# SSD's output product as seven block products a pair, with its loads, ropes and attention's start re-ordered

## The chip, the cores and the metric

The kernel runs on one core of a Trainium2 chip. The metric is the device time of one execution in microseconds (us), lower is better. Five engines work side by side, each through its own instructions in order: TensorE (PE in the profile, its weight loads PEld), VectorE (DVE), ScalarE (ACT), GpSimd (POOL) and SyncE (SP), which in this kernel issues nearly all DMAs. They wait for each other by semaphores.

## The reference

One decoder layer on 1024 tokens of width 1024, all float32: a Mamba-2 state space mixer (SSD) and differential attention side by side, merged by gates, then a gated feed-forward part. What matters here:

```python
h = rms_norm(x, pre_norm1_w[layer]) * (1.0 + sc1) + sh1
proj = h @ w_in[layer]
z, xbc, dt_raw, q, k, v, gates = jnp.split(proj, IN_SPLITS, axis=-1)
y_ssd = ssd_branch(z, xbc, dt_raw, ...)          # normed y, times norm_w
y_att = diff_attention_branch(q, k, v, ...)      # q, k rotated by rope first
gate_ssd, gate_att = jnp.split(jax.nn.sigmoid(gates), N_BRANCH, axis=-1)
merged = gate_ssd * (y_ssd @ w_ssd_o[layer]) + gate_att * (y_att @ w_attn_o[layer])
```

The change concerns `y_ssd @ w_ssd_o`, a product of 1024 x 1024 by 1024 x 1024, and what stands around it.

## The kernel before

**Numbers in two parts.** Each float32 operand is kept as a high part (rounded to fp32r by ScalarE's copy) and a low part (the rest, by VectorE's subtraction); a product is three matmuls, high by high, high by low and low by high. Tiles named `hl` hold both parts of 128 channels x 512 tokens, 4 KB a partition. h, transposed, is sixteen such tiles `hT[k][half]`, k of 8 channel groups, half of two token halves. `block_half` computes 128 output channels for 512 tokens: 8 k x 3 = 24 matmuls of 128 x 512.

**Buffers.** `Slots` is a pool of 43 buffers of 4 KB a partition. `get` takes the one that has been free longest, `put` gives one back; whoever writes a reused buffer waits for its last reader. The weights have rings of their own: raw blocks 3 deep (`wraw`), high and low parts 4 deep each.

**Pairs.** Earlier in the kernel eight pairs of 128-wide weight blocks are computed by Winograd's form of Strassen's scheme (`pairs`, `x_mms`, `x_split`, `x_sum`, loop at L618 onward): the two weight blocks and the four quarters of h (two channel halves by two token halves) give seven block products instead of eight. Each product is a step p0 to p6 of 12 matmuls. Four weight sums a pair are made by VectorE, seven weight splits by ScalarE and VectorE, and the results are gathered from three PSUM banks: X takes p0, p2, p4, p6, Z takes p1, Y takes p3 and p5. X is copied out after p0 and after p2, while the next product into X waits its turn.

```python
order = (("b11", "X"), ("b21", "Z"), ("t2", "X"), ("t1", "Y"), ("t3", "X"), ("b22", "Y"), ("t4", "X"))
```

`x_ahead(m, p)` splits the weights three steps ahead and, at two places a pair, lets SP load the next raw block (`x_load`).

**The stage of this change** lies between the SSD scan and attention, inside one block whose order on TensorE, VectorE, ScalarE and SP is written by hand. First blocks 0 and 1 of q and k (`seq`, four of them) by `block_half`, in between `turn_y`: four transposes put 128 channels of y for 512 tokens into a PSUM bank, ScalarE scales it to the high part, VectorE makes the low part. The banks are taken in the fixed rotation wa, wb, wa, wc, with two buffers of wa, so a bank is used again by the fourth turn after. After the first half of a block comes the `rope` of the block before: ScalarE's copy out of the bank, VectorE's shuffle, GpSimd's product with the cosines, VectorE's product with the sines, their sum, the split, and 16 small stores to DRAM (`store_qk`). Then the loop over eight output blocks j: 48 matmuls each, `w_ssd_o` block split ahead, gate `gsd[j]` loaded, gate times product stored to `msd[j]`. At j = 3 and 4 the q and k tiles of the first two heads are loaded (`load_qk`).

**After it** attention: a stream of dense blocks (q, k blocks 3 to 7 and the attention gates, `dense_stream`) fills TensorE between scores, transposes and values of the heads. `fill(1)` emits three matmuls. The first 14 fills come before the first score. Its order is by hand on TensorE, VectorE, ScalarE and GpSimd, while SP's instructions are placed by the scheduler there.

## Time and profile before

| | us |
|---|---|
| median of 3 runs (lowest, highest) | 1852.3 (1850.74, 1853.15) |
| profiled execution, its own time | 1848.95 |
| its span, first to last instruction | 1847.1 |
| TensorE busy in it | 1822.4 (99%) |
| VectorE, ScalarE busy | 1294.9 (70%), 888.3 (48%) |
| GpSimd busy | 144.5 (8%) |
| granted TensorE clock, mean | 0.997 |

Busy time is the time in which an engine had an instruction in work. TensorE's instructions overlap: a 128x512 matmul is shown with some 389 ns and the next one starts long before its end, so the pace is read from starts. A row of the timeline reads: start, duration, engine, line of the kernel, operation, output<-inputs, count; in brackets the engine's idle time before it and who ended it. A row of a stretch gives from:to, its length, busy time of PE, PEld, DVE, ACT and POOL with counts, the granted clock, the DMA engines' busy share, and GB/s.

### The profile page before, as it was taken

To read this page: it belongs to the slowest core of one execution; us is meant where nothing else is said; L and a number is where in the kernel's file an instruction comes from. 1 tells how busy PE (TensorE), PEld (TensorE's weight loads), DVE (VectorE), ACT (ScalarE), POOL (GpSimd) and SP (SyncE) were. 2 spreads that over 40 slices of the span, in tenths; PEclk is the share of its full clock that TensorE was granted. 3 is DMA by queue.
4 is the path that set the end of the run, shared out by engine and by line. 5 is a ranking of instruction groups with operands and counts; after the bars stand their busy time and mean duration, and the time that the engine had idled before them with its cause. 6 is when DMAs were issued, how large, how long until landed. Compare 5 with 4: busy or idle time off the path is not lost.

```text
span 1847.1 us, 24410 instructions
## 1 busy us (share of the span) xinstructions
PE 1822.4 (99%) x8974; PEld 1527.3 (83%) x8974; DVE 1294.9 (70%) x1980; ACT 888.3 (48%) x1720; POOL 144.5 (8%) x128
## 2 busy tenths in 40 slices
PE   6999999999999999999999999999999999999998
PEld 4888899988888888888888888888888888888887
DVE  6777867799654257777667464487898888876545
ACT  6644543456532145565556232565545454455532
POOL 0000000266421000000000100000000000000001
PEclk9999999999999999999999999999999999999999
DMA  8365367687646856566734754122333222378744
GB/s 335 133 216 183 103 208 238 219 315 268 242 125 185 260 132 172 165 170 164 198 104 146 236 196 177 52 95 103 103 120 108 103 97 98 109 235 309 243 158 165
DMA packets 130217, 322.57 MB, mean 175 GB/s; under 512 B 14881, under 2 KB 38833, under 8 KB 130098
## 3 DMA queue, kind: packets, MB, share of 16 engines
q1 hardware_dynamic: 129138, 317.86, 52.3%
q0 software_dynamic: 960, 3.15, 0.5%
q8 instruction: 71, 1.16, 0.3%
q14 instruction: 48, 0.39, 0.1%
HBM read 225.79 MB, written 95.17 MB: 174 GB/s over the span
## 4 chain that ended last, share of the span: by engine, by line
PE 91%; DVE 4%; ACT 3%; issue 1%; DMA 1%; POOL 0%; SPq 0%; DVEq 0%; POOLq 0%; ACTq 0%
PE upx L1744 4%; PE upx L1743 4%; PE upx L1745 4%; PE o L1437 3%; PE dx L2108 2%; PE dx L2107 2%; PE dx L2106 2%; PE upy L1743 2%; PE upy L1744 2%; PE upy L1745 2%; PE v L950 2%; PE z L117 2%; PE z L118 2%; PE z L116 2%; PE dy L2108 2%; PE dy L2107 2%
## 5 line engine op out<-in xcount | busy, mean ns | idle before, releaser
L1743 PE MATMUL upx<-t,wu_t 128*128 128x512 f32 x264 | 103.2, 391 | 0.5 <-DVE cv L2171 0.4
L1744 PE MATMUL upx<-t,wu_t 128*128 128x512 f32 x264 | 102.9, 390 | 0.2 <-DVE t L1861 0.2
L1745 PE MATMUL upx<-t,wu_t 128*128 128x512 f32 x264 | 102.7, 389 | 0.0
L1717 ACT ACTIVATE wu_t<-sab 128x512 fp32r<-128x512 f32 x57 | 34.1, 627 | 128.3 <-DVE sab L1734 128.3
L1425 ACT COPY aT<-at 128x512 f32<-128x512 f32 (+2 forms) x96 | 46.0, 479 | 96.3 <-PE at L1424 96.3
L1437 PEld LDWEIGHTS o<-vt,aT 128*128 128x128 f32 x576 | 75.3, 191 | 9.2 <-ACT aT L1425 4.6
L95 DVE TENSOR_TENSOR g_lo<-gst,g_hi 128x1024 fp32r<-128x1024 f32 (+1 forms) x42 | 47.5, 1135 | 49.0 <-ACT g_hi L94 48.9
L1437 PE MATMUL o<-vt,aT 128*128 128x128 f32 x576 | 80.9, 276 | 0.4 <-ACT aT L1425 0.2
L94 ACT ACTIVATE g_hi<-gst 128x1024 fp32r<-128x1024 f32 (+1 forms) x42 | 41.4, 988 | 63.8 <-DMA gst<-gld_s 35.8
L1398 DVE TENSOR_REDUCE nmx<-sc 128x1 f32<-128x640 f32 (+3 forms) x64 | 65.6, 1025 | 2.2
L1378 PE MATMUL sc<-kst,qst 128*128 128x512 f32 (+2 forms) x192 | 63.8, 340 | 0.0
L1379 PE MATMUL sc<-klo,qst 128*128 128x512 f32 (+2 forms) x192 | 63.3, 346 | 0.0
L1761 DVE SCALAR_TENSOR_TENSOR ug<-cg,vec,ug 128x1023 f32<-128x1023 f32 (+1 forms) x44 | 56.3, 1280 | 6.1 <-ACT ug L1760 5.3
L1743 PEld LDWEIGHTS upx<-t,wu_t 128*128 128x128 f32 x264 | 49.5, 188 | 11.6 <-DVE cv L2171 1.3
L1744 PEld LDWEIGHTS upx<-t,wu_t 128*128 128x128 f32 x264 | 49.6, 188 | 10.6 <-DVE t L1861 0.5
L1745 PEld LDWEIGHTS upx<-t,wu_t 128*128 128x128 f32 x264 | 49.6, 188 | 10.4
L1721 DVE TENSOR_TENSOR wu_t<-sab,wu_t 128x512 fp32r<-128x512 f32 x57 | 39.3, 690 | 26.6 <-ACT wu_t L1717 26.6
L1761 DVE SCALAR_TENSOR_TENSOR uv<-cv,vec,uv 128x1023 f32<-128x1023 f32 (+1 forms) x44 | 56.2, 1278 | 0.9 <-ACT uv L1760 0.9
L1414 DVE RECIPROCAL rsm<-ssum 128x2 f32<-128x2 f32 x64 | 10.6, 166 | 62.4 <-ACT p L1411 35.1
L2227 POOL TENSOR_TENSOR rsf<-rsf,nhalf 128x1 f32<-128x1 f32 x8 | 5.2, 654 | 623.5 <-DVE rsf L2226 623.5
L1416 DVE SCALAR_TENSOR_TENSOR p<-p,coef,p 128x128 f32<-128x128 f32 (+3 forms) x64 | 52.4, 819 | 2.3
L2106 PE MATMUL dx<-wdt_hi,g_hi 128*128 128x512 f32 x132 | 51.3, 389 | 0.0
(537 smaller groups left out, 5923.4 us busy)
## 6 DMA issues: line engine op xcount, KB each, us to landing
adas<-in_w_ada SPq DMA_DIRECT2D x32, 512.0 KB, 5.1
wdr<-in_w_down SPq DMA_DIRECT2D x22, 512.0 KB, 6.2
wtd<-wds SPq DMA_DIRECT2D x22, 512.0 KB, 4.6
wuf<-in_w_up SPq DMA_DIRECT2D x22, 512.0 KB, 3.5
gld_s<-gsum SPq DMA_DIRECT2D x22, 512.0 KB, 2.8
gst<-gld_s SPq DMA_DIRECT2D x20, 512.0 KB, 4.9
wdt_raw<-wtd SPq DMA_DIRECT2D x20, 512.0 KB, 5.1
wuv<-in_w_up SPq DMA_DIRECT2D x19, 512.0 KB, 3.5
```

The costliest lines, as they stand in the source:

```text
L1378: T.matmul(sc[:, n0:n1], qs_[s][:, tsl], ks_[s][:, n0:n1], start=True, stop=False)
L1379: T.matmul(sc[:, n0:n1], qs_[s][:, tsl], kl[s][:, n0:n1], start=False, stop=True)
L1398: V.reduce_max(nmx[:, bq, s : s + 1], sc[:, :L], axis=AX.X, negate=True)
L1416: V.scalar_tensor_tensor(pr[0][:, :L], pr[1][:, :L], coef[:, bq : bq + 1], pr[0][:, :L], op0=ALU.mult, op1=ALU.add)
L1437: T.matmul(po_of[j, grp][:, qi, :], at[:, k, :], vt[j % 2][:, kt, :], start=(kt == 0), stop=(kt == i))
L1743: T.matmul(out_, wh, xh_, start=(k == 0 and first), stop=False, skip_group_check=not first)
L1744: T.matmul(out_, wh, xl_, start=False, stop=False, skip_group_check=not first)
L1745: T.matmul(out_, wl, xh_, start=False, stop=(k == end), skip_group_check=not first)
L1761: V.scalar_tensor_tensor(u[:, d:], c_[:, : S - d], fw[:, 2 - d : 3 - d], u[:, d:], op0=ALU.mult, op1=ALU.add)
L2106: T.matmul(o, gh[:, kk, tsl], wh, start=(k == 0 and not more), stop=False, skip_group_check=more)
L2107: T.matmul(o, gh[:, kk, tsl], wl, start=False, stop=False, skip_group_check=more)
L2108: T.matmul(o, gl[:, kk, tsl], wh, start=False, stop=(k == KF - 1), skip_group_check=more)
```

## The change

- `w_ssd_o` leaves `seq` and becomes four more pairs, `("so", 2i, 2i+1)`, of seven products each. y's four quarters take the place of h's: `turn_y` now gives, for the first token half, the high part, a plain copy and the low part; for the second half only the difference to the first (first four channel groups) or a plain copy (last four). From these VectorE forms t2, t3, t4 and t1, and ScalarE and VectorE split them.
- The order of the q and k halves becomes (0,0), (0,1), (1,0), (1,1), (2,0), (3,0), (2,1), (3,1), where (n, half) is block n's half; the turns are spread over the first five. The differences and splits of y follow in (2,0) to (2,1) and, for b22 and t4, in the first pair's steps p1 and p3.
- The ropes of blocks 0 and 1 stay in one go; those of blocks 2 and 3 begin with a copy out of their banks (`rope_in`) and then run one instruction a step through the first two pairs.
- Buffers for all this come from h: 12 of its tiles are stored to DRAM in pairs 4 to 6 of the earlier eight (the other four were stored there already), and all 16 are loaded back (`h_back`): six in the third of the four pairs, ten in the last.
- The q and k tiles of the first two heads, their v tiles and the first two raw blocks of attention are loaded in the last pair.
- Attention's first two blocks run by halves: both first halves, then both second halves.

The core of the diff:

```diff
+    h_out = [(k, 0) for k in range(KD)] + [(k, 1) for k in range(KH, KD)]
+    hd = {kh: dp.tile([P, S], F32, tag=f"hd{kh[0]}_{kh[1]}", name=f"hd{kh[0]}_{kh[1]}") for kh in h_out}
...
+                if 4 <= m < 7 and p % 2 == 0:
+                    k, half = h_out[4 * (m - 4) + p // 2]
+                    SP.dma_start(hd[k, half], hT[k][half].rearrange("p h t -> p (h t)").bitcast(F32))
...
-    seq = [("w_q", 0), ("w_k", 0), ("w_q", 1), ("w_k", 1)] + [("w_ssd_o", j) for j in range(8)]
+    seq = [("w_q", 0), ("w_k", 0), ("w_q", 1), ("w_k", 1)]
...
+        if half == 0:
+            n, src = (("b11", y11), ("b21", y21))[c]
+            A.activation(HX[n][kk][:, 0, :], ps, AF.Copy, scale=nw)
+            V.tensor_scalar(part(src, kk), ps, nw, None, op0=ALU.mult)
+            lo_of(n, kk, src)
+        elif c == 0:
+            V.scalar_tensor_tensor(part(y12, kk), ps, nw, part(y11, kk), op0=ALU.mult, op1=ALU.subtract)
+        else:
+            A.activation(part(y22, kk), ps, AF.Copy, scale=nw)
...
+    pairs = pairs + [("so", 2 * i, 2 * i + 1) for i in range(4)]
+    turns = {(0, 0): (0, 4, 1), (0, 1): (5, 2, 6), (1, 0): (3, 7, 8), (1, 1): (12, 9, 13, 10), (2, 0): (14, 11, 15)}
...
+            if half == 0 and n in (1, 2):
+                rope_in(n - 1, qf)
+                old = rope(n - 1, qf)
+                for _ in range(5):
+                    next(old)
...
+                elif p == 1:
+                    A.copy(ev_[:, 0, :], bank["X"])
+                    if m > m0:
+                        x_sum(m, 2)
+                    x_ahead(m, 4)
+                    if m == m0:
+                        for k in range(KH):
+                            hi_of("b22", k, y22)
+                            lo_of("b22", k, y22)
...
+                elif p == 5:
+                    V.tensor_tensor(cv[:, HALF:], bank["X"], ev_[:, 0, :], op=ALU.add)
+                    x_sum(m + 1, 0)
+                    x_ahead(m, 8)
+                    out_so(1, second, cv[:, second])
...
+                if ropes is not None and next(ropes, True):
+                    assert (m, p) == (m0 + 2, 0)
...
+                if m == len(pairs) - 2 and p == 1:
+                    h_back(6)
+                if last:
+                    if p == 0:
+                        fetch(0)
+                    elif p == 2:
+                        fetch(1)
+                    elif p == 3:
+                        SL.put(*sab)
+                    SL.put(*HX[order[p][0]])
+                    if p < 3:
+                        h_back((4, 4, 2)[p])
+                    elif p == 3:
+                        qst, kst, klo = [[[SL.get(f"{n}0_{s}", F32R) for s in range(2)]] for n in ("qst", "kst", "klo")]
+                        for i in range(2):
+                            load_qk(i, qst[0][i], kst[0][i], klo[0][i])
...
+        split_later(0)
+        split_later(1)
+        for n, half in ((0, 0), (1, 0), (0, 1), (1, 1)):
+            need(("w", n))
...
+            yield from dense_half(n, half)
```

The outputs of a pair leave the banks as in the earlier pairs, and `out_so` multiplies them by the gate.

296 lines of the change are left out of this document (206 added, 90 removed).

## The prediction

> **What bounds the kernel now.** I read the page first (busy shares, the chain that ended last), then the groups on the product's tile, then stretches, then single rows for prices.
>
> ```profile
> PE 1822.4 (99%) x8974; PEld 1527.3 (83%) x8974; DVE 1294.9 (70%) x1980; ACT 888.3 (48%) x1720; POOL 144.5 (8%) x128
> PE 91%; DVE 4%; ACT 3%; issue 1%; DMA 1%; POOL 0%; SPq 0%; DVEq 0%; POOLq 0%; ACTq 0%
> ```
>
> TensorE has no slack, so a matmul that goes away is worth its pace, and anything that makes TensorE wait costs in full. The stage that changes:
>
> ```profile
> L116 PE MATMUL so<-yT,w_ssd_o_hi x128: 389/389/474, 562.1 to 649.0; 128*128 128x512 f32 x128
> L118 PE MATMUL so<-yT,w_ssd_o_lo x128: 389/389/500, 562.7 to 649.5; 128*128 128x512 f32 x128
>   DVE w_ssd_o_lo L95: 0.6, 1
> 649.69 0.39 PE L1332 MATMUL w_qp<-hT,w_q_hi 128*128 128x512 f32 x1
> 659.21 0.22 PE L1378 MATMUL sc<-kst,qst 128*128 128x128 f32 x1
> 511.40:562.10 50.70, 50.70 (x257) 42.62 (x257) 29.87 (x36) 19.36 (x29) 11.16 (x5) 1.00 0.46 125
> 200.00:220.00 20.00, 20.00 (x90) 16.58 (x89) 17.09 (x22) 10.17 (x15) 0.00 (x0) 1.00 0.38 125
> L462 PE MATMUL xx<-hT,xw_b x32: 389/389/389, 98.2 to 233.5; 128*128 128x512 f32 x32
> L464 PE MATMUL xx<-xt,xw_t x96: 389/389/389, 104.1 to 250.3; 128*128 128x512 f32 x96
> ```
>
> The reader is to see four things. The product is 384 matmuls from 562.1 to 649.7 us, with one wait of 0.6 us. Before it, blocks 0 and 1 of q and k with the transposes of y take 50.7 us, TensorE never idle, VectorE (the third figure after the span) busy 29.9. The eight pairs that use seven products already run 672 matmuls from 98.2 to 250.3, 0.2267 us each, so a pair of 84 takes 19.03 and one product (a step, p0 to p6) 2.72; VectorE is 85% busy there and TensorE never waits. The first score comes 9.5 us after the first matmul of attention's own blocks.
>
> **The change part by part.** Prices of single instructions:
>
> ```profile
> 85.03 4.90 DVE L557 TENSOR_TENSOR xt<-hr,xt 128x512 fp32r<-128x512 f32 x8
> 104.06 0.68 DVE L659 TENSOR_TENSOR xcg<-xz,xevs 128x512 f32<-128x512 f32 x1
> 524.61 2.07 DVE L1190 SCALAR_TENSOR_TENSOR yT<-ytr,vec,yT 128x512 fp32r<-128x512 f32 x3 [4.95 <-ACT yT L1189]
> 526.69 1.34 DVE L1205 STREAM_SHUFFLE sw<-qf 128x1024 f32<-128x1024 f32 x1
> 528.06 1.23 DVE L1207 TENSOR_TENSOR sw<-sw,rops 128x1024 f32<-128x1024 f32 x1
> 531.55 1.23 DVE L1208 TENSOR_TENSOR qf<-qf,sw 128x1024 f32<-128x1024 f32 x1 [2.26 <-POOL qf L1206]
> 533.90 1.23 DVE L95 TENSOR_TENSOR thlo<-qf,thhi 128x1024 fp32r<-128x1024 f32 x1 [1.13 <-ACT thhi L94]
> 535.04 1.22 DVE L95 TENSOR_TENSOR w_q_lo<-w_q_raw,w_q_hi 128x1024 fp32r<-128x1024 f32 x1
> 536.18 2.06 DVE L1190 SCALAR_TENSOR_TENSOR yT<-ytr,vec,yT 128x512 fp32r<-128x512 f32 x3
> 523.41 1.31 PE ytr L1187 x12
> ```
>
> From start to start: 0.60 us for a 128x512 VectorE op on SBUF (8 in 4.9), 0.66 for one that reads a bank, 1.14 for a 128x1024 one (533.90 to 535.04), 8.35 for a whole rope (526.69 to 535.04, waits on GpSimd and ScalarE included), 0.44 for the four transposes of one tile of y, 5.44 for a half block of 24 matmuls.
>
> *Matmuls removed.* 384 become 4 pairs x 84 = 336: 48 x 0.2267 = **-10.9 us**. The 0.6 us wait in the first output block goes with its place: **-0.6**. The 64 transposes stay.
>
> *VectorE's work added.* Per tile of y's first half a copy beside the low part; 12 differences, 28 low parts instead of 16, 16 weight sums, 28 weight splits of 0.60 instead of 8 of 1.14. ScalarE gets the matching high parts and bank copies; at 38% busy it hides them. VectorE, in order, does not, and I follow it at three places by running sums.
>
> (A) Zero is the first matmul of block 0. TensorE's second group of turns ends at 13.5, the third block half (1,0) at 18.95, its turns 3, 7, 8 at 20.25, (1,1) at 25.7, then turns 12, 9, 13, 10. VectorE: the second group from 12.8 costs 3 x 1.26 (was 3 x 0.66) to 16.6; split 17.7; rope to 26.1; then the bank reads of turns 3, 7, 8 end at 26.7, 28.0, 29.2. Turns 9, 13 and 10 take the banks of just these three, so the next block starts at 29.65 instead of 27.45: **+2.2**. Before, the turns after a rope were followed by two block halves, which hid it.
>
> (B) Zero is that next block. VectorE is free at 0.8: split 1.14 and rope to 10.3, turn 11 (0.66) and six ops of 0.60 to 14.55, 18 ops in (3,0) to 25.35, 7 in (2,1) to 29.55. In the first pair's steps p0 to p4: 0.6, 3.0, 1.26, 3.0, then a split, shuffle and product 3.1: 40.5; the bank X is added out at 41.2. TensorE: three turns 1.3, four halves 21.8, p6 at 39.4, and p6 writes X: **+1.8**. Its ends are 0 (VectorE two us ahead of my sum) and 4 (two behind). Other deadlines hold, the nearest p3's split by 0.95.
>
> (C) Rope 2 and 3 now run one instruction a step. GpSimd's product runs beside VectorE there instead of with VectorE waiting. Rows of another stage:
>
> ```profile
> 380.03 1.05 POOL L1041 TENSOR_TENSOR prev<-prev,sm 128x512 f32<-128x512 f32 x1
> 382.70 1.36 POOL L1004 TENSOR_TENSOR xdd<-xd,sm 128x512 f32<-128x512 f32 x1 [1.62 <-PE v L952]
> 383.08 1.53 DVE L719 TENSOR_TENSOR wds<-wdr,wds 128x512 f32<-128x512 f32 x1
> 395.52 0.68 DVE L719 TENSOR_TENSOR wds<-wdr,wds 128x512 f32<-128x512 f32 x1
> 528.16 3.35 POOL L1206 TENSOR_TENSOR qf<-qf,ropc 128x1024 f32<-128x1024 f32 x1 [12.85 <-issue]
> ```
>
> The same VectorE op takes 0.68 alone and 1.53 beside GpSimd, ending 0.55 after GpSimd's end (384.06). So a two-input op is held until GpSimd's product ends, 2.1 (2 x 1.05) after VectorE's own. First hold: the product ends at 40.5, GpSimd at 42.6, the weight sum in the first pair's p5 at 43.2. On to the second pair, whose p0 is at 43.9 and p6 at 60.2: VectorE's remaining p5 takes 2.34 and p6 3.0, then p0 1.86, p1 2.34, p2 3.77, to 56.5; there it is held to 58.6, then split, rope sum, split, and X out at 61.6: **+1.4** (ends 0 and 3). The page SBUF — State Buffer of the Trainium skill, section SBUF: two separate sides, calls this an exclusive lock held for the whole instruction; if the op were only slowed by the 0.85 (1.53 less 0.68) of that row, C would come to about 0.3 and the sum would be 1.1 us lower. The 1.53 row speaks for the lock.
>
> (D) SP's queue and the DMAs at the end. T is the first matmul of the last pair, so the third begins at T-19.0 and the first score is due at T+19.0+9.5 = T+28.5 (columns of the stretches: the last two are the DMA engines' share and GB/s).
>
> ```profile
> 142.00:152.00 10.00, 10.00 (x46) 8.29 (x45) 8.52 (x14) 4.70 (x8) 0.00 (x0) 1.00 1.01 394
> 148.00:150.00 2.00, 1.00 1.03 418
> 598.00:608.00 10.00, 10.00 (x46) 8.28 (x45) 1.63 (x3) 1.06 (x1) 0.00 (x0) 1.00 1.02 293
> 604.00:608.00 4.00, 4.00 (x20) 3.30 (x19) 1.63 (x3) 0.00 (x0) 0.00 (x0) 1.00 1.00 217
> 559.94 0.30 SPq L388 DMA_DIRECT2D qd<-thlo  x1
> 566.31 0.42 SPq L388 DMA_DIRECT2D qd<-thlo  x1
> qd<-thlo SPq DMA_DIRECT2D x16, 64.0 KB, 2.2
> 642.51 4.53 SPq L1357 DMA_DIRECT2D vt<-vd  x8
> ```
>
> With all DMA engines busy (share 1.0) 512 KB loads move at 394 GB/s, 1.33 us each; at 217 GB/s, 2.42 us per 512 KB, when the queue holds the k tiles' 64-row loads (the tail of a head's loads, 604 to 608). Rope 3's 16 stores move into the third pair, ahead of the fourth pair's weights and of h: 14 steps in 6.4 us, 0.455 each. (Block 2's 16 stores move into the second pair, ahead of weights due a pair later: nothing.) VectorE's lag puts the store of the second pair's output at T-15.2, SP issues it and two gates by T-13.9 and the 16 stores by T-6.6; the weight load follows (needed at T-5.4, there at about T-3: VectorE waits some 2.5 us, hidden, as its next splits are due at T+2.7), and the first of six h loads waits 2.2 for the low part's store, T-4.5. SP also waits for TensorE to end p0 and p1 before eight more h tiles, q and k queued behind; the backlog outlasts that. From there until the last low k tile of head pair 0: 16 h tiles, 2 output stores, 2 gates, 2 weight blocks and 2 q tiles = 24 x 1.33, and k as 4 x 2.42: 41.6, so T+37.1. Due T+28.5: TensorE waits **+8.5** at the first score. Lower end: 418 GB/s, the best row, and k at the mixed 293 (1.79): 24 x 1.25 + 7.2 - 4.5 = T+32.7, 4.2 late; upper end 11.6, if the next q block and the next heads' v tiles (1.33 + 1.79) get in front. Block 1's weights come at T+22 and are split about when due, T+24.5; a slip there only shortens this wait. The page DMA: Bandwidth & Descriptors of the Trainium skill, Specifications, gives a core about 358 GB/s of HBM; by it a unit is 1.46, an estimate, and D 11.8. The 394 row says otherwise.
>
> *Costed at nothing.* (E) Twelve stores of h in pairs 4 to 6: 12 x 1.33 = 16 us of DMA over 57, on a share of 0.38 (row 200 to 220): 0.66. They wait for nothing; if the cover goes, weight loads come late there, a few tenths. (F) Halves in attention's first two blocks: same matmuls, half 1 of h is due at T+30 and lands before q and k. (G) Splits of block 0 run while VectorE idles in the last pair (about 8 of 19 us used); else about 2 us, inside D's wait. (H) More h and y tiles in reused buffers: each is freed by work a step or more ahead.
>
> Sum: -10.9 - 0.6 + 2.2 + 1.8 + 1.4 + 8.5 = **+2.4 us** on the profiled execution's 1848.95 (span 1847.1 and 1.85 around it). That execution lies 3.35 below the median 1852.3; carried over, 1854.7. The measurement tells about 0.2%, 3.7 us, from no change, so I forecast no measurable change.
>
> **The rivals.**
> 1. *The loads come in time.* D under 2.4 us: -11.5 + 5.4 + at most 2.4, faster; with D zero 1846.2. For it: a leader of 3 us less VectorE lag, or k's loads not at half rate. Against: 28 units at the best rate, 1.25, need 35 us from T-4.5 and still end 2 late.
> 2. *VectorE keeps pace.* A, B, C together 0.5 and D at 4.6, its lag no longer delaying SP: -6.4, 1845.9. For it: the older pairs at 85%. Against: the banks in A are taken in a fixed order, and by the sums VectorE is busy almost without a break from turn 0 to the first pair's end.
> 3. *Slower.* The first score waits over 9.8 us: -11.5 + 5.4 + 9.8 = +3.7. One mechanism: the DMA backlog, with other loads of attention put in front of q and k on SP. At 11.6 the time is 1857.8. For it: everything that SP issues freely is issued as soon as its buffer is free, as the second heads' v loads were before (642.51). Against: that needs both groups in front.
>
> **How the numbers follow.** Forecast, D between 2.4 and 9.8: 0.40. Rival 1: 0.22, rival 2: 0.08, both faster; rival 3: 0.30. So faster 0.30, same 0.40, slower 0.30. The range takes in rivals 1 and 2 below (1846) and, above, D's 11.6 with B and C at their upper ends, 2.4 + 3.1 + 3.8, a little less: 1861. The forecast's own range is 1848.6 to 1856.
>
> **What would show it.** The product's matmuls, now on banks of another name, number 336, 19.0 us a pair. A: TensorE waits at the transposes of y after (1,1), three times, 2 us in all, for VectorE. B and C: a wait at a p6 step for VectorE's addition out of X, in the first two pairs. D: a single wait at the first score on a k tile's load, 4 to 12 us, DMA share about 1.0 from a few us before T until then. E to H: no wait of TensorE between 98 and 250 us, none at block 0's weights above 2 us. I am wrong if the wait at the first score is small, or if VectorE stalls TensorE in pairs three and four, where I see none.

## The result, and the profile after

The changed kernel takes 1868.9 us (median of four runs, 1868.6 to 1870.6) against 1851.5 (1848.7 to 1853.2): 1.0097 times the kernel before, 95% interval 1.008 to 1.0115. The forecast was 1854.7, range 1846 to 1861: wrong, on the slow side. The profiled execution has a span of 1866.9 us against 1847.1.

From the page after the change, busy shares and the chain that ended last:

```profile
PE 1822.6 (98%) x8926; PEld 1523.1 (82%) x8926; DVE 1344.2 (72%) x2060; ACT 911.4 (49%) x1768; POOL 143.3 (8%) x128
...
PE 80%; DVE 8%; DMA 6%; ACT 3%; issue 2%; POOL 1%; SPq 1%; DVEq 0%; POOLq 0%; ACTq 0%
```

TensorE has 48 matmuls less and the same busy time, and DMA, 1% of the chain before, has 6%. What TensorE waited for (us in total, times, longest one):

```profile
PE sc L1561 <- DMA kst<-khd: 5.9, 2, 4.1
...
PE sx L466 <- DVE scv L1401: 3.4, 2, 2.6
PE sc L1562 <- DMA klo<-kld: 3.1, 2, 2.0
PE w_kp L1495 <- ACT w_k_hi L1476: 2.8, 1, 2.8
...
PE ytr L1197 <- DVE ys L1202: 2.4, 2, 1.7
...
PE ytr L1197 <- DVE ys L1205: 0.7, 1, 0.7
```

The transposes of y are A, the sums in `sx` are B and C, the loads of k (`kst`, `klo`) and block 1's weights (`w_kp`) lie in D: all stand where the prediction had put them. Most of them cost more than the idle time listed here, because the granted clock fell to half behind them and the next multiplications ran slow. Stretches of the changed kernel (length; busy time of PE, PEld, DVE, ACT and POOL; PEclk, DMA share, GB/s):

```profile
539.00:552.00 13.00, 9.86 (x46) 7.86 (x45) 9.79 (x13) 4.52 (x7) 3.42 (x1) 0.87 0.45 81
608.00:612.00 4.00, 3.45 (x8) 2.70 (x9) 3.49 (x6) 1.53 (x2) 0.00 (x0) 0.59 0.57 169
640.00:648.00 8.00, 8.00 (x37) 6.64 (x36) 3.42 (x6) 2.47 (x5) 0.00 (x0) 1.00 1.01 401
660.00:668.00 8.00, 5.85 (x18) 4.20 (x17) 1.37 (x3) 0.45 (x1) 0.00 (x0) 0.79 1.05 232
668.00:676.00 8.00, 1.16 (x4) 0.89 (x5) 0.00 (x0) 0.00 (x0) 0.00 (x0) 0.63 0.78 181
676.00:680.00 4.00, 4.00 (x11) 3.13 (x11) 1.60 (x5) 1.40 (x5) 0.00 (x0) 0.50 0.93 305
```

The reader is to see two things. The granted clock is 0.87, 0.59 and 0.50 in the stretches with or just behind the waits of A, C and D, and 1.00 at 640 to 648, where nothing waits. And the DMA engines are all busy from 640 to 668, but move 401 GB/s first and 232 later.

Stage lengths, here and for all runs below, are differences of starts in the timeline. Q is q and k's stage, first `w_qp` to first `sx`; P the output product, from there to attention's first dense matmul; S from there to the sixth score (i = 5).

| kernel | Q | P | S | median us | ratio to before (95%) |
|---|---|---|---|---|---|
| before | 50.7 | 87.6 | 32.0 | 1851.5 | |
| changed | 56.0 | 81.9 | 49.0 | 1868.9 | 1.0097 (1.0080 to 1.0115) |
| e1 turns first | 50.8 | 89.0 | 49.9 | 1869.7 | 1.0104 (1.0090 to 1.0118) |
| e2 rope on VectorE | 53.4 | 79.0 | 51.6 | 1864.2 | 1.0080 (1.0066 to 1.0094) |
| e3 q, k earlier | 55.6 | 80.7 | 50.8 | 1867.7 | 1.0095 (1.0081 to 1.0109) |
| e4 k by a repeated address | | | | 2051.3 | 1.1084 (1.1069 to 1.1100) |
| e5 y copies on ScalarE | 53.2 | 81.3 | 52.0 | 1866.2 | 1.0088 (1.0075 to 1.0102) |
| e6 more fills | 55.5 | 80.9 | 59.5 | 1870.7 | 1.0111 (1.0097 to 1.0125) |
| e7 k stored twice | 55.4 | 80.9 | 42.2 | 1861.2 | 1.0058 (1.0046 to 1.0071) |
| e8 stores of h alone | | | | 1850.6 | 1.0002 (0.9993 to 1.0011) |
| e9 combined | 50.7 | 94.0 | 40.3 | 1864.5 | 1.0075 (1.0062 to 1.0089) |
| e10 TensorE kept busy | 54.5 | 81.3 | 52.2 | 1868.3 | 1.0097 (1.0083 to 1.0111) |
| e11 VectorE's side | 50.7 | 91.9 | 44.6 | 1868.3 | 1.0097 (1.0083 to 1.0111) |
| e12 ropes spread | 50.7 | 91.7 | 42.6 | 1865.0 | 1.0075 (1.0061 to 1.0089) |
| e13 ropes in steps | 50.7 | 79.1 | 45.2 | 1852.1 | 1.0007 (0.9998 to 1.0016) |
| e14 loads' side | 56.1 | 81.4 | 42.0 | 1860.2 | 1.0049 (1.0036 to 1.0061) |
| e15 slots early | 50.7 | 80.7 | 42.2 | 1854.2 | 1.0017 (1.0009 to 1.0026) |
| e16 q, k ahead | 50.7 | 81.3 | 42.9 | 1856.8 | 1.0034 (1.0021 to 1.0048) |
| e17 the same, rope at p5 | 50.7 | 80.9 | 44.7 | 1856.3 | 1.0034 (1.0022 to 1.0047) |
| e18 loads in gaps | 50.7 | P and S 118.3 | | 1850.1 | 0.9999 (0.9990 to 1.0008) |

Fills (three matmuls each, 0.68 us) borrowed ahead of the sixth score lengthen S: 18 in e6, 8 in e12 to e14, 4 in e9 and e15. They are no loss as far as attention is shorter later, but little of that is seen. In e14, against the kernel before, Q, P, S and the scan's end are 11.3 us longer, and so is the whole span (11.2), although 5.4 us of S are borrowed. In e6, with 12.2 us borrowed, the span makes up 5.0 behind the sixth score. 44 extra matmuls stand in e10's S.

The balance in the profiles: Q +5.3, P -5.6, S +17.0, together +16.7 of the spans' 19.8; the medians differ by 17.4. Of the rest, 1.7 us is the scan's end (513.1 against 511.4). Kernels with the same code up to there, but for a few small stores in some, reach it between 511.1 and 513.4, so I count it as spread. P is 11.5 short by its matmuls (4 times 19.03 is 76.1, against 87.6) and 5.8 long by waits and the halved clock behind them.

### The profile page after: what moved, and what is told of

It reads as the page before. It is cut to its first block, busy times and chain, and to the rows that moved or that the text cites. A ratio compares the mean times of both kernels' runs of the same rounds, so it can differ in the third digit from the quotient of the medians.

```text
span 1866.9 us, 24505 instructions
## 1 busy us (share of the span) xinstructions
PE 1822.6 (98%) x8926; PEld 1523.1 (82%) x8926; DVE 1344.2 (72%) x2060; ACT 911.4 (49%) x1768; POOL 143.3 (8%) x128
## 4 chain that ended last, share of the span: by engine, by line
PE 80%; DVE 8%; DMA 6%; ACT 3%; issue 2%; POOL 1%; SPq 1%; DVEq 0%; POOLq 0%; ACTq 0%
PE upx L1927 4%; PE upx L1926 4%; PE upx L1928 4%; PE o L1620 3%; PE upy L1926 2%; PE upy L1928 2%; PE upy L1927 2%; PE z L117 2%; PE z L118 2%; PE z L116 2%; PE sc L1562 2%; PE dx L2290 2%; PE ao L117 2%; PE xx L467 2%; PE ao L116 2%
## 5 line engine op out<-in xcount | busy, mean ns | idle before, releaser
L1620 PE MATMUL o<-vt,aT 128*128 128x128 f32 x576 | 80.9, 276 | 0.4 <-ACT aT L1608 0.2
L1926 PEld LDWEIGHTS upx<-t,wu_t 128*128 128x128 f32 x264 | 49.5, 188 | 11.6 <-DVE cv L2354 1.3
L1495 PE MATMUL gap<-hb,ga_hi 128*128 128x512 f32 x128 | 56.5, 441 | 0.0
```

Source lines behind the costliest of these rows:

```text
L1495: T.matmul(ps, w[0][:, k, :], xh_, start=(k == 0), stop=False)
L1620: T.matmul(po_of[j, grp][:, qi, :], at[:, k, :], vt[j % 2][:, kt, :], start=(kt == 0), stop=(kt == i))
L1926: T.matmul(out_, wh, xh_, start=(k == 0 and first), stop=False, skip_group_check=not first)
```

## The experiments

**Where the loss sits: VectorE ahead of attention.**

e1 has the bank reads ahead of the rope in (1,0):

```diff
+            if (n, half) == (2, 0): rope_now()
             for i in turns.get((n, half), ()):
                 ...turn_y(...)
+            if (n, half) == (1, 0): rope_now()
```

> The changed kernel with one order turned: after the half block (1,0) VectorE reads the banks of turns 3, 7 and 8 first and runs the rope of block 0 then. Theory: TensorE's 4.1 us of waits at the turns 9, 13 and 10 come from the 8.4 us rope ahead of those bank reads, and the 1.1 us behind them from the halved clock; q and k's stage (first w_qp to first sx) falls from 56.0 to about 51, the granted clock between 539 and 552 us stays 1.0, and the kernel takes 1864 instead of 1868.9. Rival: VectorE is simply short of time in this stage, and the wait moves to the next turns or to the first pair: the stage with the first pair's p6 (513.1 to 586.47 us, 73.4) keeps its length, 1868 to 1870.

Measured: the rival. Q is back at 50.8 with a clock of 1.00, and P is 7.1 longer; 1869.7. TensorE's waits in that run:

```profile
PE sx L466 <- DVE scv L1407: 5.4, 2, 2.9
...
PE sx L468 <- DVE xw_b L442: 2.6, 1, 2.6
PE sx L466 <- ACT yevs L1373: 1.2, 1, 1.2
```

The 5.3 us of A came back in the first pair, behind VectorE at weights and at X. A's place was a matter of order; its length was VectorE's.

e2 computes the cosine product on VectorE:

```diff
-        G.tensor_tensor(q_, q_, ropc, op=ALU.mult)
+        V.tensor_tensor(q_, q_, ropc, op=ALU.mult)
```

> The changed kernel with the rope's product with the cosines on VectorE instead of GpSimd, all four times. Theory (VectorE's two-input ops stand still as long as GpSimd's product runs): VectorE gets 1.14 us more work for each rope and loses a hold of some 2 us: the second pair's p6 wait falls from 2.75 us to under 1.2 and the halved clock behind it goes, the waits at the turns after (1,1) fall from 4.1 to about 2.8, the first pair's p6 may wait up to 2 us instead of 1.0. In all 3 to 5 us less, about 1865. Rival (the op beside GpSimd is only slower, by 0.85): VectorE gets busier by 0.3 us a rope and no wait shrinks: 1868.5 to 1871.

Measured: 1864.2, as the lock has it. The rope and the operations behind it in the second pair, from the timeline of the changed kernel (start, duration, engine, line, operation, output<-inputs, shape, count, and in brackets the idle time before with what ended it):

```profile
602.31 3.29 POOL L1226 TENSOR_TENSOR qf<-qf,ropc 128x1024 f32<-128x1024 f32 x1 [14.26 <-ACT xw_b L441]
...
603.27 2.88 DVE L442 TENSOR_TENSOR xw_t<-xwv,xw_t 128x512 fp32r<-128x512 f32 x1
...
607.81 0.68 DVE L1401 TENSOR_TENSOR scv<-sx,yevs 128x512 f32<-128x512 f32 x1
```

The same place in e2:

```profile
597.64 1.23 DVE L1226 TENSOR_TENSOR qf<-qf,ropc 128x1024 f32<-128x1024 f32 x1
...
599.92 0.68 DVE L442 TENSOR_TENSOR xw_t<-xwv,xw_t 128x512 fp32r<-128x512 f32 x1
...
602.26 0.68 DVE L1401 TENSOR_TENSOR scv<-sx,yevs 128x512 f32<-128x512 f32 x1
```

In the changed kernel a 0.68 us split lasts 2.88, from 603.27 to 606.15, which is 0.55 after GpSimd's end (602.31 + 3.29 = 605.60), and X is added out at 607.81. In e2 the product costs 1.14 from start to start, nothing is held, and the second pair has no wait (P 79.0, of which 2.0 at the first pair's p6).

e5 takes the plain copies of y off VectorE:

```diff
-            V.tensor_scalar(part(src, kk), ps, nw, None, op0=ALU.mult)
+            A.activation(part(src, kk), ps, AF.Copy, scale=nw)
```

> The changed kernel with the eight plain copies of y's first half (turn_y, half 0) made by ScalarE out of the bank instead of VectorE; nothing else moves. Theory, after the run with the turns ahead of the rope: the waits at the turns (A), at the first pair's p6 (B) and at the second's (C) are one shortage, VectorE working without a break from 513 to about 605 us, and a wait mended at one place comes back at the next. Taking 8 times some 0.75 us off VectorE then takes about 6 us off the sum: from the first w_qp to the second pair's p6 (95.4 us in the changed kernel) 89 to 91, the kernel 1861 to 1864. Rival: the places are separate, each with its order; the wait at the turns is for ScalarE's reads of the bank, which get more: the wait at the turns stays over 3 us and the kernel at 1867 to 1870.

Measured: Q 53.2 and the sum to the second pair's p6 93.6 instead of 95.4, so 1.9 us less where 4.4 to 6.4 were expected; 1866.2 lies between the theory and the rival. VectorE was not busy without a break from 513 on, as I had it: relieved, it waited 3.79 us for the next turns at 525 and then 2.29 and 1.13 inside each rope (for GpSimd's product and for ScalarE's high part). Only from about 552 to 605 does it work with hardly a break (twice 0.70 us).

**Where the loss sits: the loads.**

e3 turns the order in the last pair: q and k at p0 and p1, h's second half behind them.

```diff
-                        h_back((4, 4, 2)[p])
+                    if p == 0:   h_back(2); # q, k high part of head 0
+                    elif p == 1: # k low part of head 0, q and k of head 1
+                    elif p in (2, 3): h_back(4)
```

> The changed kernel with the order of the loads in the last pair turned: the second raw weight block of attention is loaded at p1, the q and k tiles of the first two heads at p0 and p1 in the buffers that come free there, and the eight h tiles of the second token half at p2 and p3, behind them. The bytes are the same. Theory: the first score waits for its place in the queue; with q and k ahead of half 1 the wait at it falls from 15 to 0 to 3 us, the halved clock behind it (2.2 us) goes, and half 1 of h comes in about when the dense blocks want it (0 to 3 us): 1851 to 1857. Rival: the DMA engines are short of time whatever the order, and the wait goes over to the dense blocks' h tiles of half 1 with nearly its whole length: over 1862.

Measured: the rival's time, 1867.7, with the waits at other tiles than it had named. The first score waits 2.9 us, and 9.3 us stand at two other places, block 1's weights (4.1) and the values (5.2). ScalarE's rows name the queue:

```profile
656.59 1.15 ACT L1488 ACTIVATE w_k_hi<-w_k_raw 128x512 fp32r<-128x512 f32 x2 [9.94 <-DMA w_k_raw<-in_w_k]
...
679.72 0.27 ACT L1620 COPY aT<-at 128x128 f32<-128x128 f32 x1 [10.15 <-DMA msd<-scg_b]
```

The copy `aT` writes a buffer that held the last output block, whose store now stood last in SP's queue. The queue is full, and whoever is last in it waits.

e4 loads a k tile by one DMA whose source repeats the 64 rows:

```diff
-        for r in range(2):
-            SP.dma_start(dst[64 * r : 64 * r + 64, :].bitcast(F32), src)
+        SP.dma_start(dst.bitcast(F32), src[None, :, :].broadcast_to([2, 64, S]))
```

> The changed kernel with each k tile loaded by one DMA over all 128 rows (the 64 rows in DRAM read twice by a repeated address) instead of two DMAs over 64 rows each, for all heads. Bytes written are the same. Theory: the 64-row loads are what halves the rate to some 223 GB/s from 660 to 674 us; the six q and k units of 512 KB then take 1.3 us each instead of 2.3 and the first score waits 9 us instead of 15: about 1862 to 1863. Rival: the rate is low for another cause (k and q lying in DRAM as many small rows, or two queues' worth of other loads): the rate stays under 260 GB/s, 1867 to 1870.

Measured: 2051.3 us, 11% slower, and no answer to its question. The stretch from 680 to 700 us:

```profile
680.00:700.00 20.00, 0.92 (x2) 0.57 (x2) 0.00 (x0) 0.00 (x0) 0.00 (x0) 0.50 0.20 72
```

72 GB/s at a share of 0.20. The page DMA: Bandwidth & Descriptors of the Trainium skill, Rules for kernel authors, has just this: a leading repeated dimension of c copies confines a DMA to at most c engines. The trace agrees: from 672 to 680 us, where SP issues nothing beside k's loads, the share is 0.13, that of two engines out of 16.

e7 asks the question in another way, with k stored twice for the first two heads:

```diff
                 SP.dma_start(khd[m][d0 : d0 + n, :], hi[r : r + n, :])
+                if m < 2:
+                    SP.dma_start(khd[m][64 + d0 : 64 + d0 + n, :], hi[r : r + n, :])
...
+            if m < 2: SP.dma_start(dst.bitcast(F32), src[m]); continue
```

> The changed kernel with the k of the first two heads stored twice in DRAM, for rows 0 to 63 and 64 to 127 (eight small stores more in the early pair, eight more in block 0's rope), so that each of the four k tiles of these heads is loaded by one DMA of 128 different rows. Theory: two DMAs of 64 rows after one another write to only half of the SBUF's rows at a time, and that is the low rate from 660 to 674 us (220 GB/s at a DMA share of 1.0): the six q and k units then take about 1.3 us each instead of 2.3 and the first score's wait falls from 15 to about 9: 1861 to 1864. Rival: the low rate has another cause, the rate stays under 260 GB/s: 1867 to 1870.

Measured: 1861.2 us, S shorter by 6.7. The loads at the same places as in the changed kernel:

```profile
640.00:648.00 8.00, 8.00 (x37) 6.63 (x36) 4.02 (x7) 1.74 (x3) 0.00 (x0) 1.00 1.03 409
...
660.00:664.00 4.00, 4.00 (x11) 3.13 (x10) 0.73 (x2) 0.00 (x0) 0.00 (x0) 0.50 1.03 410
```

410 GB/s where it was 232. The page SBUF — State Buffer of the Trainium skill, Door 1, says that a 64-row tile reaches half of the ports (an asymptote of some 218 GB/s); its section on two DMAs for the two halves says that they do not add up. The stretches agree: 232, though q's tiles, with all rows, are among these loads, against 410.

e6 puts 32 dense fills instead of 14 ahead of the first score and loads the second weight block at p1:

```diff
-    NFIRST, NLAST = 20, 20
+    NFIRST, NLAST = 38, 20
```

> The changed kernel with 32 instead of 14 dense fills (three matmuls each) ahead of the first score, taken off the later items' shares, and the second raw weight block loaded at p1 instead of p2. The loads are the same and in the same order otherwise. Theory: q and k of the first heads are in at T+43.5 (T, the first matmul of the last pair) whatever TensorE does, and the dense blocks have work until T+41; the first score then waits 2 to 4 us instead of 15, the 3.0 us wait for block 1's weights goes, and the halved clock behind both: 1852 to 1856. Rival: the dense work is only borrowed: it waits for its own loads (h's second half, the third block's weights) or is missing later in attention, and the kernel stays over 1862.

Measured: the rival, 1870.7. The first score still waits 5 us, and the 33rd fill waits 8.4: block 2's weights, loaded behind v, reached ScalarE at 683.3 after an idle stretch of 21.9 us. Block 1's wait went, by the load at p1.

e8 is the kernel before with the twelve stores of h.

> The kernel before with only the twelve stores of h in the pairs 4 to 6 added (nothing reads them). Theory: they cost nothing, neither in the pairs (98 to 250 us, no wait of TensorE) nor later: the time of before within 1 us. Rival: the 1.4 us that the scan's stage lost in the changed kernel comes from these stores (late loads behind them): 1.2 to 2 us slower, with the first w_qp at about 513 us instead of 511.4.

Measured: 1850.6 against 1850.3, no difference. The stretch of the eight earlier pairs, in the kernel before:

```profile
98.00:250.00 152.00, 152.00 (x672) 125.93 (x671) 123.44 (x168) 77.12 (x116) 0.00 (x0) 1.00 0.52 175
```

And in e8:

```profile
98.00:250.00 152.00, 152.00 (x673) 125.89 (x672) 123.53 (x168) 77.22 (x116) 0.00 (x0) 1.00 0.65 216
```

The DMA share rises from 0.52 to 0.65, TensorE stays at 152 of 152 us. The first `w_qp` stood at 511.9 (511.4 in the kernel before).

e10 lets TensorE compute through the wait at the first score:

```diff
+        keep = ps_wb("keep")
+        for i in range(44):
+            T.matmul(keep, splits[1][0][:, i % KD, :], hT[i % KD][0][:, 0, :], start=(i == 0), stop=(i == 43))
         probs(0, scores(0), 0)
```

> The changed kernel with 44 matmuls of 128x512 more, put ahead of the first score, into a bank that nobody reads: TensorE then computes through the 10 us in which it stands still before the first score (from about 665.4 us; the rest of D's loss lies at block 1's weights). No load moves. Theory: the granted clock falls to 0.5 for some 4 us after a wait of TensorE of more than about 2 us; without the wait it stays at 1.0 behind the first score and the kernel is 2 us faster though it computes more: 1866 to 1867.5, clock from 675 to 682 us over 0.95 (0.5 in the changed kernel). Rival: the clock falls there for another reason (the loads, the first scores): it stays at 0.5 to 0.7, 1868 to 1870.

Measured: the clock as the theory has it, the time short of it (1868.3). The stretch from 676 to 682 us, in the changed kernel:

```profile
676.00:682.00 6.00, 6.00 (x19) 4.72 (x19) 1.60 (x5) 1.40 (x5) 0.00 (x0) 0.64 0.94 324
```

And in e10:

```profile
676.00:682.00 6.00, 4.10 (x18) 3.39 (x19) 1.60 (x5) 1.29 (x5) 0.00 (x0) 1.00 0.62 214
```

From the last matmul of the first score to the second score it is 4.3 us (678.22 to 682.50), 6.5 in the changed kernel: 2.2 saved. But k's last tile came 2.6 us later (678.2 against 675.6): the 64-row loads moved 193 GB/s instead of 228 (664 to 668 us). Why is not shown. TensorE was busy there in e10 and mostly idle in the changed kernel, but in the kernel before such loads moved 217 beside a busy TensorE.

**Mending both sides.** e11 is VectorE's side alone, e9 the same with the loads' side:

```diff
         V.stream_shuffle(sw, q_, perm)
-        G.tensor_tensor(q_, q_, ropc, op=ALU.mult)
+        V.tensor_tensor(q_, q_, ropc, op=ALU.mult)
         ...
-        yield
-        yield
         A.activation(hi, q_, AF.Copy)
...
+            if half == 0 and n in (1, 2): next(old)   # rope's high and low part, behind the turns
...
-                if m == len(pairs) - 2 and p == 1: h_back(6)
+                if m == m0 + 1 and p == 5: h_back(6)      # e9 only
```

> Only part (1) of the combined kernel on top of the change: y's plain copies by ScalarE, the cosine products on VectorE, the bank reads between a rope's sum and its high part, ropes 2 and 3 from the first pair's p5 without the spare step. Theory: the waits of TensorE from the first w_qp to the last pair's start are VectorE's idle stretches inside the ropes (3.4 us each, behind GpSimd and ScalarE) and its holds beside GpSimd: q and k's stage takes 51 us instead of 56.0 and the pairs 1 to 3 57.5 instead of 62.9; rope 3's stores end a pair earlier, so that six h tiles start at about T-14 instead of T-3 and the first score waits 6 to 8 us less: 1850 to 1854. Rival: VectorE's total is what counts (2.3 us more for the cosine products in the pairs): the waits only move into the first and second pair, 1859 or more.

> The changed kernel with everything that the runs so far point to: (1) VectorE's side: y's plain copies by ScalarE; the ropes' cosine product on VectorE; turns 3, 7, 8 (and 14, 11, 15) read between a rope's sum and its high part; ropes 2 and 3 begin behind the first pair's step p5 and run without the spare step, so that they end in the second pair; (2) the loads: k of the first two heads stored twice, six h tiles loaded from the second pair's p5 instead of the third's p1, the second raw block at p1, the third before the v tiles; (3) 18 instead of 14 fills ahead of the first score. Theory: A, B and C with their halved clock go (5.3 + 1.0 + 2.75 + 1.7 = 10.7 us), and with six h tiles out of the backlog (7.7 us), full-rate k (6 us) and four more fills (2.7 us) the first score's 15.2 + 2.2 us shrink to 0 to 3: 1841 to 1846, under the kernel before. Rival: VectorE has no 6 us a rope to give in the second pair, or the h tiles of the second half come late: 1850 or more.

Measured: in both Q is 50.7 and the first pair's p6 stands at 16.3 us, not a tenth late, so A and B can be taken away. And both lose it in the second pair. TensorE in e11:

```profile
PE sx L466 <- ACT yevs L1370: 5.4, 1, 5.4
PE sx L466 <- ACT yevs L1385: 5.0, 1, 5.0
```

ScalarE's copies of X stood behind a rope's high part, which waited for VectorE (first) and for the stores of the rope before (second). I had taken out the change's spare step, and that step was what kept ScalarE free. In e9 S is down to 40.3, but six h tiles in front of the output's store make VectorE wait 9.3 us for its buffer in the third pair.

e12 places each part of ropes 2 and 3 by hand behind the copies, e13 keeps the change's steps, e14 has the loads' side alone (k twice, second weight block at p1, third ahead of v, 8 more fills):

```diff
+        plan = {(0, 5, 0): 2, (1, 1, 0): 2, (1, 2, 1): 2, (1, 3, 1): 23, ...}      # e12
...
-    NFIRST, NLAST = 20, 20
+    NFIRST, NLAST = 28, 20
```

> The changed kernel with the sequential part and the loads of the combined one, and ropes 2 and 3 placed by hand: rope 2's products and sum in the first pair's p5, behind the addition out of X and ahead of the gate product; its high part in the second pair's p1 behind the copy of X, low part p2, stores p3; rope 3's first half at p3, the rest in p5 behind the addition out of X, its high part in the third pair's p1 behind the copy of X, low part p2, stores p3, and the six h tiles behind them. k of the first two heads twice, 22 fills ahead of the first score. Theory: the two 5 us waits of the combined kernel were ScalarE's copies of X queued behind a rope's high part that waited for VectorE or for the stores of the rope before; placed behind the copies they cost nothing: the four pairs take 76 to 78 us (91 in the combined kernel, 82 in the changed one), the first score waits 0 to 2, the kernel takes 1840 to 1844. Rival: VectorE has no time for two ropes in the first two pairs, and X waits for it at p6 wherever the ropes stand: pairs over 80 us, 1847 or more.

> As the kernel with the ropes placed by hand, but ropes 2 and 3 in the change's own steps (start at the first pair's p4, a spare step before the high part), with the cosine product on VectorE. Theory (order on ScalarE and in front of X): the start of rope 2 ahead of the addition out of X costs 2 us at the first pair's p6, as in the run with the cosines on VectorE alone, and nothing else: pairs 78 to 79 us, 1842 to 1846. Rival (VectorE's time): over 80 us, 1847 or more.

> Only the loads' side of it on top of the change: k of the first two heads stored twice, the second raw block loaded at p1, the third ahead of the v tiles, 22 instead of 14 fills ahead of the first score. Theory: A, B and C stay as in the changed kernel (q and k's stage 55 to 56 us, pairs 81 to 82), while the first score, now due 34 us after the last pair's start with its tiles there at some 38, waits 3 to 4 us and block 1 no more: from the last pair's end to the sixth score 40 to 42 us with the borrowed fills (49.0 in the changed kernel, 32.0 in the one before), 1853 to 1857. Rival: the dense blocks run into their own loads, as with 32 fills: over 1860.

Measured: e12's first three pairs take 57.4 us (three times 19.03 is 57.1), so VectorE does have the time. Then the last pair waits 12.6 us: a v load of the second heads, which the scheduler had put into SP's queue, held it from 619.3 to 631.7; six h tiles and then the store of an output came behind it, and VectorE stood still for that store:

```profile
649.02 0.69 DVE L1420 TENSOR_TENSOR scv<-sx,yevs 128x512 f32<-128x512 f32 x1 [18.15 <-DMA msd<-scv]
```

e13 hits P (79.1, one wait of 1.8 at the first pair's p6) and misses its time, 1852.1 for 1842 to 1846, because q and k come 40 us after the last pair's start. It is 16.9 us faster than the change and level with the kernel before. e14 has P and Q as expected and S at 42.0, but 1860.2: of the borrowed fills nothing is seen to come back later (the balance above).

e15 gives four rope buffers back a pair earlier, e16 adds the order of e3 and the change's 14 fills, e17 starts rope 2 at p5:

```diff
+                if (m, p) == (m0 + 1, 4):
+                    SL.put(ropc, rops, sw, qf)
+                    h_back(4)
```

> As the kernel with the ropes in their own steps (e13), but the four buffers that rope 3 no longer needs after its sum (cosines, sines, shuffle, rope 2's data) are given back in the second pair's p4 and take four h tiles there, at a DMA share of 0.5 to 0.7; two h tiles stay in the third pair. 18 fills ahead of the first score instead of 22. Theory (start of the loads): the q and k tiles come four units, 5.2 us, earlier, at about 658; the first score, due at 654, waits 3 to 4 us: 1847 to 1850. Rival (total of the DMA engines): other loads fill the place and nothing comes earlier: 1852 to 1854.

> On top of the early buffers: in the last pair q and k of the first head at p0, the rest at p1, the v tiles and two h tiles at p2, six h tiles at p3, so that the eight h tiles of the second half come last; 14 fills ahead of the first score as in the change. Theory: with the backlog 5 us shorter, k at full rate and this order, q and k are in 22 us after the last pair's start (due 28.5), the k-th tile of h's second half at 23.3 + 1.29 k (due from 31 on): no wait of TensorE behind the pairs, 1841 to 1845, under the kernel before. Rival: as in the run that only turned this order (e3), the wait goes over to h's second half and the v tiles: over 1848.

> The one before with rope 2's start behind the addition out of X in the first pair's p5 instead of ahead of it. Theory: the 2 us at the first pair's p6 go, all four pairs in 77 us: 1839 to 1843. Rival: VectorE, 2 us further behind, keeps ScalarE and X waiting in the second pair instead: as the one before or slower.

Measured: all three miss. In e15 q and k came at 662.5 instead of 663.2: SP stood behind the third pair's output store until 631, so the early tiles only left a gap. In e16 the first score was on time (9.5 us after the first dense matmul, as before the change), and 5.4 us stood at the values. There the profile names no releaser for ScalarE's copy `aT`, but the copy starts 0.07 us after the landing of the last output's store, at 669.30, so it is the wait of e3 again; in e17 it is the same (670.50 and 670.56). In e17 the first pair's p6 is on time, and most of the gain is lost again in the second pair (21.6 us instead of 19.0). In e15 and e16 the first pair takes 1.6 us more than in e13, though the wait at its p6 is the same (1.83 and 1.81): the clock fell there and not in e13 (below).

e18 is e16 with the v tile loaded in the second pair, five h tiles in the third, rope 3's stores behind that pair's weight load, and in the last pair the loads of p0 ahead of the third pair's output stores:

```diff
+                    if last:
+                        fetch(0)
+                        h_back(3)
+                        ...                                  # q of the first head
+                        SP.dma_start(msd[j - 2], cgv[0])
```

> As the kernel with q and k ahead of h's second half (e16), with its loads moved into gaps: the v tile of the first heads is loaded in the second pair's p4, in one of the buffers that rope 3 gives back, five h tiles in the third pair's p1, rope 3's stores stand behind the weight load of that step, and in the last pair the loads of p0 (weights, three h tiles, q) stand ahead of the stores of the third pair's outputs. Theory (start and order): DMA work goes on from the last pair's p0 on, 3.5 us earlier, without v's slow loads; q and k are in 21 us after the pair's start, h's second half from 22 to 31; no wait of TensorE behind the pairs over 1 us, the sixth score 32 to 34 us after the last pair's end (42 to 43 in the runs before, 32.0 in the kernel before): 1842 to 1847, under the kernel before. Rival: VectorE's and SP's queue are what is full; moving a load only moves the wait (VectorE's for a gate, a store or a weight block in the third pair): 1850 or more.

Measured: 1850.1 us, level with the kernel before (0.9999, 0.9990 to 1.0008), 18.8 below the change, missing its 1842 to 1847. From the first `w_qp` to the sixth score it needs 169.0 us (before 170.2, changed 186.9). 24 matmuls of block 0 run ahead of the last p6 in it, so P and S are not told apart. One long wait is left:

```profile
662.67 0.27 ACT L1638 COPY aT<-at 128x128 f32<-128x128 f32 x1 [8.02 <-DMA msd<-scg_b]
```

It is the copy `aT` again, in the buffer of the last output, whose store stood behind h's second half. Another buffer for it was not tried. Of the 11.5 us that the matmuls save, 1.2 arrive at the sixth score; the rest is lost to TensorE's waits: 2.0 at the first pair's p6, 0.8 in the second pair, 4.5 at this copy and 1.7 by the halved clock behind it, 0.9 at block 1's weights. So no version here beats the kernel before; the two best equal it.

## Why the prediction was wrong

| term | predicted | measured | shown by |
|---|---|---|---|
| matmuls and the old wait | -11.5 | -11.5 | P of e12's first three pairs |
| A, turns | +2.2 | 4.1, and 1.1 of clock | e1, e11 |
| B, first p6 | +1.8 | 1.0 | e9, e11 |
| C, second p6 | +1.4 | 2.75, and 1.7 of clock | e2 |
| D, first score | +8.5 | 15, and 2 of clock behind it | e7, e3, e18 |
| E, stores of h | 0 | 0 | e8 |

*The step that failed is D*, the wait for the loads: 8.5 us predicted, 15 measured. T, the first matmul of the last pair, is at 632.06. The landings of the loads in the trace split the difference into three terms.

- The start, 1.3: the first h load was issued at T-3.2, not T-4.5.
- The beginning of the backlog, 3.3: I let it run at the full rate from that issue on. But the weight block in front of it landed only at 630.70, from 628 to 632 the DMA engines moved 240 to 254 GB/s at a share of 0.82 to 0.85, and the second h tile was in 5.96 us after the first one's issue instead of 2.66. From there to the 21st of the 22 units (512 KB each) ahead of q and k (634.84 to 660.08) the pace was the predicted 1.33 a unit.
- The 64-row loads, 1.7: the last h tile and the six units of q and k took 15.4 us (660.08 to 675.48) instead of 13.7. I gave the h tile and q's two the full rate, but in one queue with the 64-row loads the h tile took 2.14 and q's second tile 2.59.

e7 takes the 64-row loads away: its six units of q and k took 7.8 us instead of 13.3, and S fell by 6.7. Block 1's weights, expected at T+22, came at T+26.7 with the same late start. The order was right (the tiles of the first score are last), and so was the price of a full-rate unit (512 KB at 401 to 410 GB/s are 1.28 to 1.31 us, predicted 1.33). Rival 3, the DMA backlog in front of the first score, is what happened, by its mechanism though not by its other loads, and beyond its 9.8 and 11.6.

*A whole term was missing: the clock.* The prediction had put it at nothing. Behind the waits of A and C and behind block 1's weights the granted clock was 0.50 for 3.4 us, and from 670.1 to 680.4 around the first score's last waits. That cost 1.1 (A), 1.7 (C) and 2 (behind the first score), and 1.8 more inside D, behind block 1's weights. The page before showed the half clock only at the kernel's start, and I had no row of a wait in mid-kernel. The page TensorE: Matmul & The Clock Gate of the Trainium skill, Part 1, ties the fall to an idle window of some 3.4 us that runs free of the kernel. The traces agree with the window's length, as the clock changes only on a grid of 3.41 us; but a window need not be idle throughout, 1.95 us of it were always enough (last section). I should have priced that rule as a rival. How large the term came out was partly chance: C's wait stands with 2.5 to 2.6 us in nine runs (the changed kernel, e1, e3 to e7, e10, e14), and the clock fell behind it in four (the changed kernel, e1, e4, e14).

*A* came out 1.9 us larger, most of it for two reasons. VectorE's second group of turns began 13.6 us after the stage's first matmul instead of 12.8, as its first read waits for ScalarE's, and a turn took VectorE 1.39 from start to start instead of 1.26:

```profile
526.71 0.75 DVE L1202 TENSOR_SCALAR ys<-ytr,vec 128x512 f32<-128x512 f32 x1 [2.54 <-ACT yb L1201]
...
528.11 0.74 DVE L1202 TENSOR_SCALAR ys<-ytr,vec 128x512 f32<-128x512 f32 x1
...
540.42 0.75 DVE L1202 TENSOR_SCALAR ys<-ytr,vec 128x512 f32<-128x512 f32 x1
...
541.81 0.74 DVE L1202 TENSOR_SCALAR ys<-ytr,vec 128x512 f32<-128x512 f32 x1
```

The bank reads ended at 541.2, 542.6 and 543.9, and TensorE's next turn followed each one. *B* came out smaller because A's longer wait had let VectorE catch up; by e1 the two are one debt. *C* was right in its mechanism, the hold until GpSimd's product ends (both held operations end 0.55 us behind it), and 1.3 us too small: VectorE reached the second hold 13.9 us after the second pair's start (589.37) instead of 12.6, because it had stood still twice for 0.70 us, for ScalarE's high parts, which the sum had left out. The first hold and the two waits:

```profile
586.34 2.27 DVE L450 TENSOR_TENSOR ysab<-xwv 128x512 f32<-128x512 f32 x1
...
592.84 0.69 DVE L442 TENSOR_TENSOR xw_t<-ysab,xw_t 128x512 fp32r<-128x512 f32 x1 [0.70 <-ACT xw_t L441]
...
597.77 0.69 DVE L442 TENSOR_TENSOR xw_t<-ysab,xw_t 128x512 fp32r<-128x512 f32 x1 [0.70 <-ACT xw_t L441]
```

*E* held, e8. *F* had no run of its own; in its two blocks TensorE waits for weights and nothing else. *G* held: at block 0's weights TensorE does not wait. The 2.8 us at block 1's are the slip of that load, which D had named and which shortens the wait at the first score. The prediction's own marks were good: A at the turns, C at a p6, D at the first score with a DMA share of 1.0. Only "a single wait at the first score" was not; it was four, and one at block 1's weights. Rival 1 is out: in the changed kernel the loads were 15 us late, and in e6 still 5 after 18 more fills (12.2 us of matmuls). Rival 2 is out by e2: there VectorE's waits cost some 5.5 us less, and S stayed at 51.6.

## What to carry to other kernels

Price each new wait of TensorE above about 1.8 us with up to 1.7 us more for the halved clock behind it, half of a stretch of 3.41 us; it does not come each time (four of nine waits of some 2.5 us had it). When a change moves work in front of a stage with a full DMA queue, add up what is in the queue until its last member lands and ask who waits for that one, stores and reused buffers included: here a better order alone (e3) only picked another victim. Where one engine works in order for two others (here VectorE, and ScalarE behind it), a wait taken away comes back at the next deadline unless its work or its own idle time shrinks; find the idle time inside its chains first.

## What the runs showed of the hardware

*The granted clock changes only on a grid of 3.41 us, and TensorE's idle time inside one stretch of the grid decides.* In every trace the moments at which the clock changes lie whole multiples of 3.413 us apart, and where the grid lies against the kernel's stages differs from run to run. Over the 20 traces (from 60 us on, without the last 25) a stretch at full clock was followed by 0.50 in all 47 cases in which TensorE idled for 1.95 us or more of it, in 6 of the 16 cases between 1.65 and 1.95, and never below. The clock came back to 1.00 behind a stretch with at most 0.55 us idle, and did not with 0.60 or more. So the length of a wait alone does not decide. The longest wait without a fall that I found is e1's of 2.85 us in front of the first pair's p6 (585.0 to 587.8), which an edge at 586.51 cuts in two:

```profile
583.10:586.51 3.41, 1.86 (x9) 1.21 (x7) 3.38 (x6) 0.39 (x1) 0.47 (x1) 1.00 0.84 284
586.51:589.92 3.41, 2.10 (x9) 1.75 (x10) 3.41 (x4) 0.00 (x0) 2.90 (x1) 1.00 0.39 159
589.92:593.33 3.41, 3.41 (x17) 2.82 (x16) 3.41 (x6) 0.00 (x0) 0.00 (x0) 1.00 0.00 0
```

C's wait of 2.58 us in the changed kernel lies inside one stretch, of which 0.83 us are busy:

```profile
605.28:608.69 3.41, 0.83 (x5) 0.37 (x4) 3.41 (x5) 0.00 (x0) 0.32 (x1) 1.00 0.77 137
608.69:612.10 3.41, 3.41 (x9) 2.63 (x10) 2.80 (x5) 1.63 (x3) 0.00 (x0) 0.50 0.54 173
```

At A three shorter waits, 1.68, 0.73 and 0.73, put 2.1 us idle into one stretch (540.43 to 543.84). The difference between e13 and e15 is of the same kind. The wait in front of the first pair's p6, in the timeline of e13:

```profile
581.38 0.50 PE L470 MATMUL sx<-yt,xw_t 128*128 128x512 f32 x1 [1.81 <-DVE scv L1412]
581.71 0.40 PE L471 MATMUL sx<-yt,xw_t 128*128 128x512 f32 x1
581.95 0.39 PE L472 MATMUL sx<-yt,xw_t 128*128 128x512 f32 x1
```

And in that of e15:

```profile
581.49 0.62 PE L470 MATMUL sx<-yt,xw_t 128*128 128x512 f32 x1 [1.83 <-DVE scv L1412]
581.91 0.63 PE L471 MATMUL sx<-yt,xw_t 128*128 128x512 f32 x1
582.33 0.63 PE L472 MATMUL sx<-yt,xw_t 128*128 128x512 f32 x1
```

In e13 an edge at 580.08 leaves 0.5 us of the wait on one side and 1.3 on the other, and TensorE goes on at 0.24 a matmul (581.71 to 581.95). In e15 the 1.83 us lie inside one stretch (578.31 to 581.72), and it goes on at 0.42. Of seven runs with a wait of 1.81 to 1.84 at this place (e2, e5, e10, e13, e15, e16, e18) the clock fell in two, e15 and e16, for 3.4 us, at a cost of 1.6; in e18, with 1.82 inside one stretch, it did not.

*A 64-row load slows the full-row loads beside it in the queue* (in the changed kernel the last h tile took 2.14 us and q's second tile 2.59, against 1.33 for the units before), and *loads with a repeated leading dimension left the DMA engines at a share of 0.20* (72 GB/s in e4).

*One core's loads ran at 406 GB/s for 28 us* (632 to 660 in the changed kernel). That is above the 358 that the prediction weighed, from the Specifications of the page DMA: Bandwidth & Descriptors of the Trainium skill; the row was the better guide.
